# Layer 0's front in another order: twelve convolution taps and the norms' sums of squares on TensorE, other blocks' norms later

## The chip, the cores and the metric

The kernel runs on one core of a Trainium2 chip. The time of a run is the device time of one execution in microseconds (us). Engines are named as in the profile: PE is TensorE's matmuls, PEld its weight loads, DVE is VectorE, ACT is ScalarE, POOL is GpSimd, SP the queue that issues the DMAs.

## What is computed

Two layers of a streaming encoder, on 1024 prompt frames and 8 x 16 sample frames of 1024 channels:

```
h = rms_norm(x, g1)                          # x * rsqrt(mean(x*x) + eps) * g
q, k, v, a, b = split(h @ w_in)
u = a * sigmoid(b)
A = sliding_window_attention(rope(norm(q)), rope(norm(k)), v, sinks)
C = silu(layer_norm(causal_depthwise_conv31(u) + conv_b))
x = x + concat(A * beta_a, C * beta_c) @ w_out
h = rms_norm(x, g2)
x = x + square(relu(h @ w_up)) @ w_down
```

The depthwise convolution has 31 taps and 512 channels: each output column is the sum of 31 shifted columns of `u`, each times one weight per channel, plus a bias. Everything is float32.

## The kernel before

Channels lie on the 128 partitions and frames along the free axis. The 1152 frames are three blocks (`b` = 0, 1, 2) of 384; the last holds the sample frames. A product of the projections is made of three matmuls per 128 rows (`gemm`, L213 to L215): weights and activations are each split into a rounded float32r part and a rest, and hi x hi, hi x lo and lo x hi are summed. A unit is one 128-column piece of a projection, 24 such matmuls; its weights come in two half units (`half_unit`), each a DMA into one of four `raw` tiles, a cast on ScalarE (L205) and a subtraction on GpSimd (L206), here called a split, into one of six `w` tiles.

A layer's front does, for each block: `rmsnorm`; `glu` (8 units for a and b, then `u` on GpSimd); `make_qkv` (6 units); the attention in chunks of 64 queries (scores L525, softmax on VectorE and ScalarE, transposes L550, values L560); the convolution (`conv`); `out` (8 units of the output projection `w_out`, and the second norm); then the feed-forward network. Attention and convolution are generators that stand in lanes beside the projections; after every unit `tick` advances them by the rates in `ATT` and `CONV`, and a list scheduler then sets each engine's order. Every engine works off its queue in order.

The convolution runs on VectorE alone. For each of 4 channel tiles a PSUM tile `c` takes 31 taps, one instruction each (L345 for the first, with the bias, then L347), and ScalarE copies it back over `u` (L350). `conv_tail` makes the layer norm of it, with one fp32 matmul for the mean (L651) and three for the variance.

`rmsnorm` squares pairs of 128-channel rows on ScalarE (L260) into tiles `f`, of which there are two, adds them on VectorE (three of L264, then L265), and sums over the partitions with three matmuls by a column of ones (L241). `rsqrt` makes the inverse root of 128 x 3 numbers on GpSimd: a power (L231) and four small steps (L232 to L235). Three transposes spread it over the partitions (L247), and VectorE and ScalarE write the normalised block in two parts (L275, L276, L277).

In layer 0 the order is: load blocks 0 and 1, norms of both; `glu` of block 0 (its convolution starts beside it); norm of block 2; `make_qkv` of 0 and 1; attention of 0 to its end, then of 1 beside what follows; `glu` of 1 and 2; `out` of 0 with its second norm; feed-forward of block 0 in the background; `make_qkv` of 2; and on. It is in `run`:

Of the kernel before, what the change touches and what calls it, by code (L numbers as in the profile page):

```python
# [37 lines left out]
CONV = ((6, 5, 3), (3.5, 3.5, 3.5))  # L38
TAIL = (3, 2)
ATT = ((0.5, 0.3, 0.3), (0.3, 0.35, 0.25))  # L40
# [21 lines left out]
class Kernel:  # L62
# [160 lines left out]
    def rsqrt(self, v, shape, scale=1.0):  # L223
# [8 lines left out]
        nc.gpsimd.tensor_tensor(out=t, in0=y, in1=v, op=ALU.mult)  # L232
        nc.gpsimd.tensor_tensor(out=t, in0=t, in1=y, op=ALU.mult)
        nc.gpsimd.tensor_scalar(out=t, in0=t, scalar1=-0.5 * scale, scalar2=1.5 * scale, op0=ALU.mult, op1=ALU.add)
        nc.gpsimd.tensor_tensor(out=r, in0=t, in1=y, op=ALU.mult)  # L235
# [14 lines left out]
    def rmsnorm(self, x, l, gcol):  # L250
        for h in self.rmsnorm_steps(x, l, gcol):
            pass
        return h

    def rmsnorm_steps(self, x, l, gcol):
# [9 lines left out]
        nc.vector.tensor_tensor(out=acc[:, 0], in0=acc[:, 0], in1=acc[:, 1], op=ALU.add)  # L265
        yield
        R, spare = self.pr()
        r = self.token_rsqrt(spare[:, :NB], acc[:, 0], C_O1024)
# [57 lines left out]

    def conv(self, l, b):
# [3 lines left out]
        for ct in range(4):  # L331
# [8 lines left out]
            for k in range(CW):  # L340
# [8 lines left out]
                if k == CW - 1:  # L349
                    nc.scalar.copy(u[:, :BT], acc)  # L350
# [663 lines left out]
    def run(self):  # L1014
# [10 lines left out]
        x.append(self.load_x(src[1]))  # L1025
        h1 = [self.rmsnorm(x[b], 0, G1) for b in range(2)]
        for l in range(DEPTH):
# [16 lines left out]
            def out(b):  # L1044
# [3 lines left out]
                if b < NB - 1:  # L1048
                    h[b] = self.rmsnorm(x[b], l, G2)

            with tc.tile_pool(name=f"ap{l}", bufs=1) as self.ap:
# [3 lines left out]
                if l == 0:  # L1055
                    for n in ("sk", "sv", "sc"):
                        self.after(nc.sync.dma_start(a[n + "o"], a[n + "old"]), self.mark)
                    h1.append(self.rmsnorm(self.load_x(src[2]), l, G1))
                attention(0, self.make_qkv(l, 0, h1[0]))
                if l:  # L1060
                    self.glu(l, 1, h1[1], conv)
                qf = self.make_qkv(l, 1, h1[1])
                self.finish("attention")
                attention(1, qf)
                if not l:
                    self.glu(l, 1, h1[1])
                    self.side("conv", self.conv(l, 1), conv[1])
                if l:
# [192 lines left out]
```

## Time and profile before

| | us |
|---|---|
| median of 3 runs (2408.23 to 2409.8) | 2408.95 |
| the profiled execution | 2407.56 |
| its span, first to last instruction | 2405.8 |
| TensorE busy in the span | 2319.9 (96%) |
| VectorE busy | 1658.2 (69%) |
| ScalarE busy | 1270.5 (53%) |
| GpSimd busy | 1530.3 (64%) |

Busy is the share of the span in which an engine worked on at least one instruction. The busy time of TensorE contains stretches at a lower granted clock: its clock has two levels, 1.2 and 2.4 GHz, and the profile gives the mean granted share of the higher one. In a timeline a row is an instruction or a run of like ones: start, length, engine, line, operation, output<-input, shape, count, and in brackets the idle time of the engine before it and what ended it. A plain fp32 matmul leaves two records.

### The profile page before, as it was taken

How to read it: one execution, taken by the hardware profiler on the slowest of the kernel's cores; microseconds unless marked ns; L12 is line 12 of the kernel's file. 1: busy time of each engine (PE TensorE's matmuls, PEld its weight loads, DVE VectorE, ACT ScalarE, POOL GpSimd, SP SyncE). 2: the span in 40 equal slices, each digit the busy share in tenths (PEclk: the TensorE clock that was granted, in tenths of full speed). 3: DMA queues.
4: the chain of work that ended last, by engine and by line, in shares of the span. 5: the costliest groups of instructions: out<-in, count | busy, mean ns of one | idle time of the engine just before them, and what ended most of it. 6: DMA issues, size and time to landing. Idle time of an engine off the chain costs nothing.

```text
span 2405.8 us, 38983 instructions
## 1 busy us (share of the span) xinstructions
PE 2319.9 (96%) x13822; PEld 2254.8 (94%) x13822; DVE 1658.2 (69%) x2993; ACT 1270.5 (53%) x2732; POOL 1530.3 (64%) x1375
## 2 busy tenths in 40 slices
PE   6999898999999999999999999999999999999999
PEld 6898798999998999999999999999999899999999
DVE  4999887996368777686687764599834877752222
ACT  5467555555435555554566467466443555544442
POOL 5885566566467666766865776856445666676662
PEclk9999899999999999999999999999999999999999
DMA  5422433334332222544333344334333122244442
GB/s 179 139 92 93 122 96 110 111 107 138 110 97 78 68 71 80 164 122 134 101 119 108 114 155 134 128 105 124 97 101 118 55 70 75 84 162 136 132 127 75
DMA packets 164260, 266.49 MB, mean 111 GB/s; under 512 B 24753, under 2 KB 55729, under 8 KB 164017
## 3 DMA queue, kind: packets, MB, share of 16 engines
q1 hardware_dynamic: 164064, 264.01, 35.5%
q8 instruction: 108, 1.77, 0.3%
q14 instruction: 88, 0.71, 0.1%
HBM read 250.19 MB, written 16.05 MB: 111 GB/s over the span
## 4 chain that ended last, share of the span: by engine, by line
PE 76%; DVE 16%; POOL 3%; issue 2%; DMA 2%; ACT 2%; SPq 0%; DVEq 0%; POOLq 0%; ACTq 0%
PE g L715 14%; PE g L213 13%; PE g L215 13%; PE g L214 13%; DVE c L347 5%; PE x L998 4%; PE x L918 4%; PE g L998 3%; PE g L918 2%; PE m L715 2%; PE r L715 2%; POOL w L885 1%; PE c L715 1%; DMA A<-in_w 1%; PE s L525 1%
## 5 line engine op out<-in xcount | busy, mean ns | idle before, releaser
L206 POOL TENSOR_TENSOR w<-raw,w 128x512 fp32r<-128x512 f32 x728 | 965.6, 1336 | 592.3 <-ACT w L205 572.7
L205 ACT CAST w<-raw 128x512 fp32r<-128x512 f32 x728 | 445.6, 620 | 457.6 <-PE g L715 134.6
L213 PE MATMUL g<-h,w 128*128 128x384 f32 x1696 | 576.4, 340 | 7.2 <-ACT h L276 3.8
L214 PE MATMUL g<-h,w 128*128 128x384 f32 x1696 | 573.1, 338 | 1.1 <-DVE h L277 1.1
L215 PE MATMUL g<-h,w 128*128 128x384 f32 x1696 | 573.4, 338 | 0.0
L347 DVE SCALAR_TENSOR_TENSOR c<-u,vec,c 128x384 f32<-128x384 f32 (+1 forms) x960 | 498.5, 519 | 19.0
L715 PE MATMUL g<-hid,w 128*128 128x384 f32 x2304 | 431.2, 341 | 9.3 <-DVE x L717 6.3
L715 PEld LDWEIGHTS g<-hid,w 128*128 128x128 f32 x2304 | 399.6, 189 | 17.8 <-DVE x L717 10.8
L213 PEld LDWEIGHTS g<-h,w 128*128 128x128 f32 x1696 | 320.8, 189 | 11.4 <-ACT h L276 4.6
L214 PEld LDWEIGHTS g<-h,w 128*128 128x128 f32 x1696 | 320.6, 189 | 2.8 <-DVE h L277 2.0
L215 PEld LDWEIGHTS g<-h,w 128*128 128x128 f32 x1696 | 320.4, 189 | 0.7
L699 DVE TENSOR_TENSOR hid<-t,hid 128x384 fp32r<-128x384 f32 x128 | 106.3, 831 | 197.4 <-ACT hid L698 197.2
L885 POOL TENSOR_TENSOR w<-S,w 128x512 fp32r<-128x512 f32 x96 | 138.5, 1446 | 120.0 <-ACT w L884 119.7
L717 DVE TENSOR_TENSOR x<-x,g 128x384 f32<-128x384 f32 x240 | 129.8, 549 | 77.0 <-PE g L715 76.7
L696 ACT ACTIVATE t<-g 128x384 f32<-128x384 f32 x128 | 62.9, 491 | 143.7 <-PE g L215 142.5
L998 PE MATMUL x<-F,w 128*128 128x384 f32 x624 | 119.2, 336 | 3.4 <-DVE x L1001 2.4
L885 POOL TENSOR_TENSOR w<-raw,w 128x512 fp32r<-128x512 f32 x64 | 90.6, 1416 | 41.0 <-ACT w L884 39.7
L998 PEld LDWEIGHTS x<-F,w 128*128 128x128 f32 x624 | 109.4, 188 | 4.9 <-DVE x L1001 2.5
L998 PE MATMUL g<-F,w 128*128 128x384 f32 x528 | 108.3, 340 | 4.1 <-ACT F L807 1.4
L884 ACT CAST w<-S 128x512 fp32r<-128x512 f32 x96 | 59.7, 622 | 96.1 <-DVE S L871 51.1
L998 PEld LDWEIGHTS g<-F,w 128*128 128x128 f32 x528 | 92.6, 188 | 8.4 <-ACT F L807 2.7
L885 POOL TENSOR_TENSOR w<-A,w 128x512 fp32r<-128x512 f32 x64 | 87.0, 1364 | 18.6 <-ACT w L884 18.4
(227 smaller groups left out, 4016.8 us busy)
## 6 DMA issues: line engine op xcount, KB each, us to landing
raw<-in_w SPq DMA_DIRECT2D x792, 256.0 KB, 2.7
A<-in_w SPq DMA_DIRECT2D x64, 256.0 KB, 2.8
x<-in_x SPq DMA_DIRECT2D x24, 384.0 KB, 4.8
x<-xd SPq DMA_DIRECT2D x12, 384.0 KB, 5.2
kept<-x SPq DMA_DIRECT2D x4, 768.0 KB, 4.0
x<-kept SPq DMA_DIRECT2D x8, 384.0 KB, 4.7
xd<-x SPq DMA_DIRECT2D x4, 768.0 KB, 3.5
out_y<-x SPq DMA_DIRECT2D x4, 768.0 KB, 4.7
```

The lines of the kernel that those rows point to most:

```text
L205: nc.scalar.copy(u[:, 0], raw)
L206: nc.gpsimd.tensor_tensor(out=u[:, 1], in0=raw, in1=u[:, 0].bitcast(F32), op=ALU.subtract)
L213: nc.tensor.matmul(ps, lhsT=u(0, k), rhs=h(0, k), start=k == 0, stop=False)
L214: nc.tensor.matmul(ps, lhsT=u(0, k), rhs=h(1, k), start=False, stop=False)
L215: self.pe = nc.tensor.matmul(ps, lhsT=u(1, k), rhs=h(0, k), start=False, stop=k == KT - 1)
L347: t = nc.vector.scalar_tensor_tensor(out=o, in0=src(k), scalar=w, in1=o, op0=ALU.mult, op1=ALU.add)
L699: nc.vector.tensor_tensor(out=hid[:, 1], in0=f, in1=hid[:, 0].bitcast(F32), op=ALU.subtract)
L715: self.pe = nc.tensor.matmul(ps, lhsT=u(p), rhs=hid[:, q], start=i == 0, stop=i == n - 1)
L717: nc.vector.tensor_tensor(out=x[:, m], in0=x[:, m], in1=ps, op=ALU.add)
L885: nc.gpsimd.tensor_tensor(out=u[:, 1], in0=f[n], in1=u[:, 0].bitcast(F32), op=ALU.subtract)
L918: nc.tensor.matmul(ps, lhsT=u[:, p, k], rhs=H[h](q, k), start=start and k == 0 and i == 0, stop=k == 3 and i == 2, skip_group_check=True)
L998: nc.tensor.matmul(o, lhsT=u[:, p, 2 * i + j], rhs=F(j, hn)[:, q], start=start and n == 0, stop=n == 5, skip_group_check=True)
```

## The change

The convolution of block 0 in layer 0 does its first 12 taps on TensorE, as 12 matmuls with a diagonal matrix of the tap's weights, in two groups of six; VectorE builds the diagonals from the identity (`diagonal`) and adds the other 19 taps to the same PSUM tile; the bias moves to ScalarE's copy. In five norms of layer 0 (`pe=True`) each square is summed by TensorE, 24 matmuls by the column of ones instead of VectorE's four additions and 3 matmuls. In the first norm the four small steps behind the power run on VectorE. Block 1 is loaded and normed after `glu` of block 0, block 2 after `out` of block 0; `glu` of 1 comes before `make_qkv` of 1; `out` of 0 comes before `glu` of 2; the feed-forward of block 0 starts before `glu` of 2. The rates of attention 1 rise from 0.3 to 0.4. Layer 1 keeps its order.

```diff
+TAPS = ((12, 0, 0), (0, 0, 0))
-ATT = ((0.5, 0.3, 0.3), (0.3, 0.35, 0.25))
+ATT = ((0.5, 0.4, 0.3), (0.3, 0.35, 0.25))
...
-        nc.gpsimd.tensor_tensor(out=t, in0=y, in1=v, op=ALU.mult)
...
+        eng = eng or nc.gpsimd
+        eng.tensor_tensor(out=t, in0=y, in1=v, op=ALU.mult)
...
+        if pe:
+            R, spare = self.pr()
+            nc.vector.memset(spare[:, :NB], 0.0)
         for i in range(0, KT, 2):
             sq = self.two()
             nc.scalar.activation(sq, x[:, i:i + 2], AF.Square)
-            if acc is None:
+            if pe:
+                for k in range(2):
+                    for j in range(NB):
+                        nc.tensor.matmul(spare[:, j:j + 1], lhsT=sq[:, k, j * 128:(j + 1) * 128], rhs=self.cst[:, C_O1024:C_O1024 + 1],
+                                         start=False, stop=i + k == KT - 1, skip_group_check=True)
+            elif acc is None:
...
+    def diagonal(self, l, ct, k0):
+
+        d = self.hp.tile([128, 2, BT], F32R, tag="hid", name=self.nm("dg"), bufs=4).bitcast(F32).rearrange("p a b -> p (a b)").rearrange("p (k c) -> p k c", c=128)
+        w = self.v(l, CWT + ct * CW + k0, 6)
+        self.nc.vector.tensor_tensor(out=d, in0=self.ident.unsqueeze(1).to_broadcast([128, 6, 128]), in1=w.unsqueeze(2).to_broadcast([128, 6, 128]), op=ALU.mult)
+        self.diagonals.append(d)
...
-            for k in range(CW):
+            taps = TAPS[l][b]
+            for k0 in range(0, taps, 6):
+                if ct == 0 and k0 == 0:
+                    yield
+                dg = self.diagonals.pop(0)
+                for k in range(6):
+                    self.pe = nc.tensor.matmul(acc, lhsT=dg[:, k], rhs=u[:, k0 + k:k0 + k + BT], start=k0 + k == 0, stop=k0 + k == taps - 1)
+                if 2 * ct < 4:
+                    self.diagonal(l, ct + 2, k0)
+                yield
+            for k in range(taps, CW):
...
-        x.append(self.load_x(src[1]))
-        h1 = [self.rmsnorm(x[b], 0, G1) for b in range(2)]
+        self.diagonals = []
+        h1 = [self.rmsnorm(x[0], 0, G1, True, nc.vector)]
+        for ct in range(2):
+            for k0 in range(0, TAPS[0][0], 6):
+                self.diagonal(0, ct, k0)
...
                 if l == 0:
+                    h1.append(self.rmsnorm(self.load_x(src[1]), l, G1, True))
+                    attention(0, self.make_qkv(l, 0, h1[0]))
+                    self.glu(l, 1, h1[1])
+                    self.side("conv", self.conv(l, 1), conv[1])
                     for n in ("sk", "sv", "sc"):
                         self.after(nc.sync.dma_start(a[n + "o"], a[n + "old"]), self.mark)
...
+                    qf = self.make_qkv(l, 1, h1[1])
+                    self.finish("attention")
+                    attention(1, qf)
+                    out(0)
+                    h1.append(self.rmsnorm(self.load_x(src[2]), l, G1, True))
+                    self.back, self.mix = self.feed_forward(l, range(alone), [blk(0)]), mix[1]
+                    self.glu(l, 2, h1[2])
```

Three places show how the engines' queues change. The first is GpSimd's queue at the start, before (L231 to L235 are the first norm's power and its four steps on tiles `s`, L206 the weights' splits):

```order
L231 TENSOR_TENSOR s_120<-s_118,half 128x3
L206 TENSOR_TENSOR w_216<-raw_215,w_216 128x512
L232 TENSOR_TENSOR s_121<-s_120,s_118 128x3
L206 TENSOR_TENSOR w_221<-raw_220,w_221 128x512
L206 TENSOR_TENSOR w_250<-raw_249,w_250 128x512
L233 TENSOR_TENSOR s_121<-s_121,s_120 128x3
L206 TENSOR_TENSOR w_255<-raw_254,w_255 128x512
L206 TENSOR_TENSOR w_305<-raw_304,w_305 128x512
L234 TENSOR_SCALAR s_121<-s_121 128x3
L206 TENSOR_TENSOR w_310<-raw_309,w_310 128x512
L235 TENSOR_TENSOR s_122<-s_121,s_120 128x3
```

And with the change (the split is L207 there, the power L232):

```order
L207 TENSOR_TENSOR w_186<-raw_185,w_186 128x512
L207 TENSOR_TENSOR w_191<-raw_190,w_191 128x512
L207 TENSOR_TENSOR w_220<-raw_219,w_220 128x512
L207 TENSOR_TENSOR w_225<-raw_224,w_225 128x512
L207 TENSOR_TENSOR w_288<-raw_287,w_288 128x512
L207 TENSOR_TENSOR w_293<-raw_292,w_293 128x512
L232 TENSOR_TENSOR s_133<-s_131,half 128x3
```

The power has moved behind the first six splits, and the four steps have left this queue.

The second place is TensorE's queue where the output projection of block 0 begins (it multiplies `ao`, the attention's output; `p` and `pt` are an attention chunk's probabilities before and after the transpose, `s` the scores), with the change:

```order
L585 MATMUL m_1946<-cst,p_1918 128x128
L585 MATMUL m_1946<-cst,p_1919 128x128
L595 MATMUL m_1946<-pt_1939,v_981 128x256 x6
L595 MATMUL m_1946<-pt_1947,v_981 128x256 x3
L560 MATMUL s_2441<-k_888,q_1645 128x64 x6
L560 MATMUL s_2441<-k_1983,q_1645 128x128 x6
L214 MATMUL g_2167<-ao_1068,w_2169 128x384
L214 MATMUL g_2210<-ao_1068,w_2212 128x384
```

Before, the same projection began right behind a unit of block 2's `glu` (`h_607`) and one chunk's transposes:

```order
L214 MATMUL g_2674<-h_608,w_2715 128x384
L215 MATMUL g_2674<-h_607,w_2715 128x384
L550 MATMUL m_2026<-cst,p_2006 128x128
L550 MATMUL m_2026<-cst,p_2007 128x128
L213 MATMUL g_2769<-ao_1034,w_2771 128x384
L213 MATMUL g_2870<-ao_1034,w_2872 128x384
```

The last chunks of the first attention now stand between the last unit of block 1 and the projection that needs them, with no unit among them.

The third place is TensorE's queue after that projection, up to the next unit. Before, one norm (its sums L241, its broadcast L247) and parts of two chunks stand there, with the keys' sums (L374) of block 2's first unit; then come the feed-forward's first unit (`h_3248`) and block 2's next (`h_607`):

```order
L374 MATMUL g_3274<-cst,t_3309 128x2 x3
L241 MATMUL r_3231<-cst,f_3219 128x1 x3
L560 MATMUL m_2648<-pt_2641,v_1369 128x256 x6
L560 MATMUL m_2648<-pt_2649,v_1451 128x256 x3
L550 MATMUL m_2838<-cst,p_2818 128x128
L550 MATMUL m_2838<-cst,p_2819 128x128
L247 MATMUL r_3231<-cst,s_3239 128x128 x3
L213 MATMUL g_3331<-h_3248,w_3333 128x384
L213 MATMUL g_3377<-h_607,w_3379 128x384
```

With the change, this is the end of a piece of 41 rows without a unit, with two norms' sums (L270) and broadcasts (L249) and most of four chunks:

```order
L270 MATMUL r_2777<-cst,f_2803 128x1 x6
L595 MATMUL m_3015<-pt_3008,v_1994 128x256 x6
L595 MATMUL m_3015<-pt_3016,v_2075 128x256 x3
L249 MATMUL r_2777<-cst,s_2815 128x128 x3
L585 MATMUL m_3203<-cst,p_3183 128x128
L585 MATMUL m_3203<-cst,p_3184 128x128
L214 MATMUL g_2849<-h_2824,w_2852 128x384
L214 MATMUL g_2850<-h_2824,w_2886 128x384
L214 MATMUL g_2933<-h_2750,w_2935 128x384
```

The first unit behind it is block 2's (`h_2824`, from the second of the two norms); the feed-forward's (`h_2750`, from the first) stands behind it.

## Rows read from the trace of the kernel before

**Rows 1.** The page, busy time, share of the span, instructions.

```profile
PE 2319.9 (96%) x13822; PEld 2254.8 (94%) x13822; DVE 1658.2 (69%) x2993; ACT 1270.5 (53%) x2732; POOL 1530.3 (64%) x1375
```

**Rows 2.** Busy time by stretches: PE, PEld, DVE, ACT, POOL; granted clock, DMA share, GB/s.

```profile
0.00:25.00 25.00, 2.37 (x10) 1.88 (x10) 5.75 (x10) 9.19 (x12) 11.18 (x19) 1.00 0.68 240
25.00:190.00 165.00, 158.72 (x1021) 151.06 (x1021) 146.12 (x264) 95.30 (x219) 131.21 (x133) 0.97 0.37 119
190.00:310.00 120.00, 105.03 (x636) 97.90 (x636) 108.62 (x203) 74.45 (x184) 57.16 (x61) 0.91 0.35 102
310.00:400.00 90.00, 83.15 (x521) 77.81 (x520) 66.15 (x125) 43.66 (x84) 68.54 (x80) 0.98 0.37 115
400.00:550.00 150.00, 145.68 (x887) 140.48 (x886) 142.52 (x324) 92.11 (x257) 85.23 (x82) 0.99 0.36 109
550.00:2405.80 1855.80, 1824.96 (x10755) 1785.67 (x10754) 1189.08 (x2072) 955.75 (x1979) 1177.02 (x1001) 1.00 0.35 109
```

**Rows 3.** Timeline of the start: start us, length us, engine, line, operation.

```profile
11.30 1.44 PE L241 MATMUL r<-cst,f 128*128 128x1 f32 x6 [11.30 <-DVE f L265]
...
13.10 0.86 POOL L231 TENSOR_TENSOR s<-s,half 128x3 f32<-128x3 f32 x1 [10.23 <-DMA raw<-in_w]
13.93 1.26 POOL L206 TENSOR_TENSOR w<-raw,w 128x512 fp32r<-128x512 f32 x1
...
21.74 0.19 POOL L235 TENSOR_TENSOR s<-s,s 128x3 f32<-128x3 f32 x1
...
22.93 2.19 DVE L275 SCALAR_TENSOR_TENSOR f<-x,vec,r 128x384 f32<-128x384 f32 x4 [9.98 <-PE r L247]
...
24.98 1.33 PE L213 MATMUL g<-h,w 128*128 128x384 f32 x3 [2.09 <-ACT h L276]
```

**Rows 4.** Busy time, clock, DMA share and GB/s while the first loads run.

```profile
2.00:14.00 12.00, 1.44 (x6) 1.36 (x6) 3.68 (x6) 4.29 (x6) 1.77 (x4) 1.00 0.97 364
```

**Rows 5.** TensorE's timeline at a plain fp32 matmul among projections.

```profile
214.09 0.81 PE L651 MATMUL r<-f,cst 128*128 128x384 f32 x2
214.44 0.63 PE L215 MATMUL g<-h,w 128*128 128x384 f32 x1
214.91 0.33 PE L213 MATMUL g<-h,w 128*128 128x384 f32 x1
```

**Rows 6.** TensorE's timeline at a norm's three sums among projections.

```profile
41.32 0.72 PE L241 MATMUL r<-cst,f 128*128 128x1 f32 x6
41.90 0.42 PE L214 MATMUL g<-h,w 128*128 128x384 f32 x1
```

**Rows 7.** VectorE from 25 to 420 us, groups: count | busy us, mean ns | idle before.

```profile
L347 DVE SCALAR_TENSOR_TENSOR c<-u,vec,c 128x384 f32<-128x384 f32 x240 | 148.4, 618 | 4.3
L277 DVE TENSOR_TENSOR h<-f,h 128x768 fp32r<-128x768 f32 x16 | 17.7, 1114 | 0.1
L275 DVE SCALAR_TENSOR_TENSOR f<-x,vec,r 128x384 f32<-128x384 f32 x29 | 16.2, 609 | 9.0 <-PE r L247 8.9
...
L264 DVE TENSOR_TENSOR f<-f,f 128x768 f32<-128x768 f32 x10 | 11.7, 1168 | 3.6 <-ACT f L260 3.6
...
L265 DVE TENSOR_TENSOR f<-f 128x384 f32<-128x384 f32 x3 | 4.1, 1375 | 0.0
```

**Rows 8.** TensorE's timeline in block 0's output projection.

```profile
241.92 1.33 PE L213 MATMUL g<-co,w 128*128 128x384 f32 x3 [5.05 <-ACT co L640]
```

**Rows 9.** TensorE's timeline after that projection, at block 0's second norm.

```profile
290.31 0.38 PE L550 MATMUL m<-cst,p 128*128 128x128 f32 x2
...
293.25 1.33 PE L560 MATMUL m<-pt,v 128*128 128x256 f32 x9 [0.23 <-DVE pt L552]
295.10 0.80 PE L550 MATMUL m<-cst,p 128*128 128x128 f32 x4 [0.52 <-DVE og L564]
298.09 0.90 PE L247 MATMUL r<-cst,s 128*128 128x128 f32 x3 [2.19 <-POOL s L235]
...
301.08 1.01 PE L213 MATMUL g<-h,w 128*128 128x384 f32 x2 [1.67 <-ACT h L276]
```

More of the change, by code (lines that the diff above doesn't have):

```diff
@@ L264, in rmsnorm_steps @@
                 nc.vector.tensor_tensor(out=acc, in0=acc, in1=sq, op=ALU.add)
-        nc.vector.tensor_tensor(out=acc[:, 0], in0=acc[:, 0], in1=acc[:, 1], op=ALU.add)
+        if not pe:
+            nc.vector.tensor_tensor(out=acc[:, 0], in0=acc[:, 0], in1=acc[:, 1], op=ALU.add)
         yield
-        R, spare = self.pr()
-        r = self.token_rsqrt(spare[:, :NB], acc[:, 0], C_O1024)
+        if pe:
+            r = self.rsqrt(self.plus_eps(spare[:, :NB], [NB]), [NB], eng=eng)
+        else:
+            R, spare = self.pr()
+            r = self.token_rsqrt(spare[:, :NB], acc[:, 0], C_O1024)
         yield
@@ L349, in conv @@
                 if k == CW - 1:
-                    nc.scalar.copy(u[:, :BT], acc)
+                    if taps:
+                        nc.scalar.activation(u[:, :BT], acc, AF.Identity, bias=self.v(l, CB + ct))
+                    else:
+                        nc.scalar.copy(u[:, :BT], acc)
                 yield
@@ L1048, in out @@
                 if b < NB - 1:
-                    h[b] = self.rmsnorm(x[b], l, G2)
+                    h[b] = self.rmsnorm(x[b], l, G2, not l)
             with tc.tile_pool(name=f"ap{l}", bufs=1) as self.ap:
@@ L1055, in run @@
                 if l == 0:
+                    h1.append(self.rmsnorm(self.load_x(src[1]), l, G1, True))
+                    attention(0, self.make_qkv(l, 0, h1[0]))
+                    self.glu(l, 1, h1[1])
+                    self.side("conv", self.conv(l, 1), conv[1])
                     for n in ("sk", "sv", "sc"):
                         self.after(nc.sync.dma_start(a[n + "o"], a[n + "old"]), self.mark)
-                    h1.append(self.rmsnorm(self.load_x(src[2]), l, G1))
-                attention(0, self.make_qkv(l, 0, h1[0]))
-                if l:
-                    self.glu(l, 1, h1[1], conv)
[L1062 to L1068, printed above, removed]
+                    qf = self.make_qkv(l, 1, h1[1])
[5 more added lines that the diff above has]
+                    self.glu(l, 2, h1[2])
+                else:
+                    attention(0, self.make_qkv(l, 0, h1[0]))
+                    self.glu(l, 1, h1[1], conv)
+                    qf = self.make_qkv(l, 1, h1[1])
+                    self.finish("attention")
+                    attention(1, qf)
                     out(0)
@@ L1072, in run @@
                     self.glu(l, 2, h1[2])
-                else:
-                    self.glu(l, 2, h1[2])
-                    out(0)
-                self.back, self.mix = self.feed_forward(l, range(alone), [blk(0)]), mix[1]
+                    self.back, self.mix = self.feed_forward(l, range(alone), [blk(0)]), mix[1]
+                if l == 0:
+                    self.finish("attention")
                 qf = self.make_qkv(l, 2, h1[2])
```

14 lines of the change are left out of this document (7 added, 7 removed).

## The prediction

> **What bounds the kernel now.** I read the page first: TensorE is busy 96% of the span, the next engine 69% [rows 1]. Then the table by stretches [rows 2], which shows where the missing time lies. Before 25 us TensorE does nearly nothing. From 550 us on it is busy 1825 of 1856 us at a granted clock of 1.00, one matmul every 0.17 us (1855.8 over 10755): whatever is late at 550 us is late at the end, one for one. Between 25 and 550 us, the part that the change rewrites, it is idle 6.3 + 15.0 + 6.9 + 4.3 = 32.4 us, and the granted clock falls short by 0.03 x 165 + 0.09 x 120 + 0.02 x 90 + 0.01 x 150 = 19.1 us. So some 51.5 us are all that any reordering of this part can give back. In the same stretches VectorE is full: 146.1 + 108.6 of the 285 us from 25 to 310, 89%. That is what the change relieves, and it does so by giving TensorE more work.
>
> **The change, part by part.**
>
> *The start.* Before, the four small steps after the power (`L232` to `L235`) stand on GpSimd between weight splits of 1.26 us each, so that 8.6 us pass from the power at 13.10 to the last step at 21.74, and the first product of the norm on VectorE starts at 22.93 [rows 3]. The change moves these four to VectorE, each some 0.2 us, but the power itself now stands behind six splits. The splits wait for weights, and the DMA engines are full until the weights come: 0.97 of 16 engines from 2 to 14 us [rows 4]. Without the second block's 1.57 MB at 364 GB/s ahead of them the weights come 4.3 us earlier; the fifth and sixth still wait for a raw buffer. I put the sixth split's end at 16, the power's at 17, four steps and the broadcast at 18.9: **-4 us**. The squares' sums run on TensorE, idle then; at the half clock a record takes 0.24 us (1.44 us for six [rows 3]), so 48 of them take 11.5 us from the arrival of the constants at some 7.5 us, and the gain would be 0.5; with sums and weights both early it is 6.
>
> *Taps on TensorE.* 4 channel tiles x 12 = 48 matmuls of 128x384 in plain fp32. The nearest row has just this form, the mean of the convolution's tail: two records, and from its start to the projection after the next 0.82 us, of which the projection between takes its usual 0.17: 0.65 us [rows 5]. 48 x 0.65 = **+31 us**, in the stretch where TensorE has projections to do; nothing covers it. The upper bound has half of them behind waits, at 1.2 GHz, where each takes twice: 24 x 0.65 + 24 x 1.3 = 47 us. Nothing in the rows makes one cheaper.
>
> *Sums on TensorE.* 24 matmuls instead of 3 in each of five norms. Six records took 0.58 us at full clock, 0.10 each [rows 6]; half of the 0.24 at half clock is 0.12. I take 0.11: 48 records are 5.3 us against 0.6, 4.7 more. The first norm's lie in the idle start, two lie in the stretch after the first output projection (below), and two cost in full: **+9.4 us** (8 to 10).
>
> *VectorE's relief.* 48 taps x 0.618, and for each norm 3 x 1.168 + 1.375 = 4.9 us [rows 7]; eight diagonals of 128x768 come back at about 1.1 each (by the sum of two 768 wide tensors in the same rows; 0.9 to 1.2), four of them in the empty start. From 25 to 310 us that is 30 + 15 - 4 = 40 us less of 255: VectorE falls from 89% to about 75%. This is worth nothing by itself, only as TensorE's waits on VectorE grow shorter.
>
> *The order.* The first output projection now comes after four groups of projections, not five: block 2's (8 units, 24 matmuls each) follows it. Two places of TensorE's queue change.
> (a) Ahead of the output projection nothing but attention is left. Before, it began between projections and then waited 5.05 us for the convolution's output, and its next three products took 1.33 us, at half clock [rows 8]. That wait goes: the tail now ends well ahead. In its place stand the last two chunks of the first attention. A chunk's end, from its last transposes to the next one's first, took 4.8 us when TensorE had little else (290.31 to 295.10 [rows 9]); two such ends and their first transposes take about 12 us, of which some 7 are matmuls that have to be done anyway: **+5 us** (3 to 10).
> (b) After it, two norms follow each other and TensorE's first product is block 2's, which needs the second. Before, one norm stood there and 10.8 us passed from the last product of the projection before to the next (290.31 to 301.08), 7.8 of it up to the broadcast at 298.09 [rows 9]. Now: 7.8 to the first broadcast; then the products of the first norm, 8 x 0.609 + 4 x 1.114 = 9.3 us of VectorE [rows 7], hold the two tiles that the second norm's squares need; then again 7.8 and 3.0: 28 us. Against 10.8 that is 17 more. Three chunks' attention products run in it, which before lay among projections: 1.33 us for the product with the values and 0.8 for four transposes [rows 9], about 6 us in all. The two norms' sums are inside it too: **+11 us** (5 to 17).
>
> *What comes back.* Of the 51.5 us I leave 2 for the cold start of the first products (1.33 us for three, from 24.98 [rows 3]) and 8 for that norm's stall, which (b) counts. 41 remain: waits on VectorE or on the convolution's tail [rows 8], and the half clock behind them. With a quarter of VectorE free instead of a tenth, I let three quarters go: **-30 us** (20 to 45).
>
> *Against the skill.* Busy time of matmuls, by which I counted the slack, shows TensorE 32.4 us idle from 25 to 550 us, the weight loads' column (PEld) 165 - 151.1 + 120 - 97.9 + 90 - 77.8 + 150 - 140.5 = 57.7 [rows 2]. The Trainium skill ("Perfetto Trace Analysis", Identifying the Most-Contended Engine) says that matmul busy time is a bad measure and that the weight loads' share is a good one. By it there would be 25 us more to give back, and at the same share the sum would be 15 us lower. The trace speaks for most of the smaller figure: after 550 us, where TensorE is full, PEld too is idle 3.8% of the time, which is 20 us in 525.
>
> **Sum.** -4 + 31 + 9.4 + 5 + 11 - 30 = +22.4. The profiled execution took 2407.56 us (span 2405.8), so it comes to 2430; the median of the three runs is 1.4 higher, 2408.95, which gives **2431 us**. Adding the terms' bounds in quadrature (3 at the start, 6 for taps, 12 for what comes back, 6 and 3 for the two stretches) gives some 15 either way for this case alone, 2417 to 2446.
>
> **Rivals.** About 0.2%, 4.8 us, is what a measurement of this kernel can tell from no change.
> - *VectorE was the true limit (faster).* It is 89 to 95% busy in the stretches from 25 to 310 us and from 400 to 550 us, and a tap ahead in its queue holds up the softmax behind it. If all of TensorE's slack but the cold start returned (49 us) and the two new stretches cost no more than the old ones: -4 + 31 + 9.4 - 49 = -12.6, 2396 us. It decides only if over 36 us come back beside free stretches; TensorE would then be full from 21 us on, which it is in no stretch before 400 us [rows 2]. Against it speaks the queue order: both new stretches are chains through VectorE, ScalarE and GpSimd. 0.10.
> - *The sides cancel.* 45 us come back, (a) costs 3, (b) 5: +0.4, 2409 us. 0.10.
> - *More slack than TensorE's row shows* (the weight loads' measure above): 15 us lower, 2416 us. 0.05.
> - *The new order waits more than I count.* The chains of (a) and (b) reach their upper bounds, 10 and 17, and only 20 come back: -4 + 31 + 9.4 + 10 + 17 - 20 = +43, 2452 us. 0.05.
> - That the change doesn't do what it says is excluded: the queues hold 48 taps and 153 - 48 = 105 more sums.
>
> **How the numbers follow.** My forecast has 0.70. Faster by over 0.2% is the first rival, 0.10; within 0.2% the second, 0.10; the forecast, the third and the fourth are slower, 0.80. The range leaves out the first rival and the outer part of the last, 2408 to 2450.
>
> **What would show it.** In the profile after: the first projection at about 21 us; 96 records of the taps at 0.32 us from one to the next in full streams; TensorE's busy sum about 45 to 50 us higher; VectorE's about 45 lower; a stretch of some 28 us after the output projection of block 0 without a projection; the wait on the convolution's output there gone. The stretch from 400 us on should only be shifted. I am wrong if TensorE's idle and cold time up to 550 us falls under 20 us, or if the taps run in fewer than 0.65 us each.

## The result, and the profile after

The changed kernel takes **2452.8 us** (median of 4 runs, 2448.28 to 2455.11), the kernel before 2409.19 in the same comparison: a ratio of **1.0176, 95% interval 1.0164 to 1.0188**, 43.6 us slower. Forecast was 2431 with a range of 2408 to 2450. The direction was right, and the size was half of what came. The profiled execution has a span of 2451.6 us.

The page's busy line of the changed kernel answers to [rows 1]:

```profile
PE 2390.3 (97%) x14128; PEld 2316.6 (94%) x14128; DVE 1610.7 (66%) x2942; ACT 1273.5 (52%) x2732; POOL 1525.8 (62%) x1371
```

TensorE is busy 70 us more (forecast 45 to 50), VectorE 47.5 us less (forecast 45). The same stretches as in [rows 2], with the same columns:

```profile
0.00:25.00 25.00, 12.55 (x55) 11.86 (x56) 9.96 (x17) 9.72 (x13) 12.50 (x16) 1.00 0.67 226
25.00:190.00 165.00, 165.00 (x959) 147.65 (x959) 105.73 (x193) 78.43 (x182) 99.80 (x102) 0.99 0.29 98
190.00:310.00 120.00, 106.35 (x645) 98.63 (x643) 85.92 (x182) 71.07 (x179) 52.62 (x55) 0.74 0.26 86
310.00:400.00 90.00, 88.28 (x518) 87.37 (x517) 63.10 (x96) 45.66 (x86) 57.78 (x58) 0.99 0.38 114
400.00:550.00 150.00, 148.80 (x934) 140.68 (x932) 100.39 (x235) 79.07 (x181) 97.60 (x106) 0.98 0.34 111
550.00:2451.60 1901.60, 1869.35 (x11027) 1830.39 (x11026) 1245.60 (x2222) 989.55 (x2096) 1205.53 (x1034) 1.00 0.33 109
```

Up to 190 us TensorE is full, as it was in no such stretch before, and VectorE is far from it (64%). Counted as the prediction counted it, the slack from 25 to 550 us is 16.6 us of idle time and 0.01 x 165 + 0.26 x 120 + 0.01 x 90 + 0.02 x 150 = 36.8 us that the clock falls short, 53 us together, against 51.5 before (32.4 idle, 19.1 of clock). In sum no slack has gone. It was spread before, and now most of it lies between 190 and 310 us, where the granted clock is 0.74.

Two pieces of TensorE's queue without a unit are there. The first is (a), ahead of block 0's output projection. TensorE's timeline:

```profile
207.74 0.34 PE L216 MATMUL g<-h,w 128*128 128x384 f32 x1
...
212.69 1.01 PE L585 MATMUL m<-cst,p 128*128 128x128 f32 x4
218.56 0.69 PE L585 MATMUL m<-cst,p 128*128 128x128 f32 x2 [4.86 <-DVE pt L587]
...
220.74 2.29 PE L595 MATMUL m<-pt,v 128*128 128x256 f32 x9
...
228.95 2.29 PE L595 MATMUL m<-pt,v 128*128 128x256 f32 x9 [1.25 <-DVE pt L587]
...
234.20 1.01 PE L214 MATMUL g<-ao,w 128*128 128x384 f32 x2
```

It lasts 26.3 us (forecast 12). The second is (b), between that projection and block 2's first unit, 42.1 us (forecast 28):

```profile
271.31 0.34 PE L216 MATMUL g<-co,w 128*128 128x384 f32 x1
...
272.43 2.34 PE L270 MATMUL r<-cst,f 128*128 128x1 f32 x18
...
287.76 0.90 PE L249 MATMUL r<-cst,s 128*128 128x128 f32 x3
...
291.38 2.29 PE L595 MATMUL m<-pt,v 128*128 128x256 f32 x9 [2.30 <-DVE pt L587]
...
297.43 5.28 PE L270 MATMUL r<-cst,f 128*128 128x1 f32 x24 [0.30 <-ACT f L266]
...
303.04 5.12 PE L270 MATMUL r<-cst,f 128*128 128x1 f32 x24
...
310.57 0.90 PE L249 MATMUL r<-cst,s 128*128 128x128 f32 x3 [0.29 <-POOL s L237]
...
313.57 0.79 PE L214 MATMUL g<-h,w 128*128 128x384 f32 x3 [1.42 <-ACT h L291]
```

The two norms follow each other as forecast: the second broadcast (L249) comes 22.8 us after the first. The table by stretches for just these two shows what they cost:

```profile
208.00:234.20 26.20, 17.26 (x123) 14.37 (x122) 19.86 (x47) 12.58 (x35) 17.82 (x23) 0.59 0.14 48
271.50:313.50 42.00, 36.79 (x196) 33.84 (x195) 22.93 (x58) 27.30 (x73) 5.49 (x13) 0.55 0.21 69
```

The second looks 88% busy, but at a granted clock of 0.55, that is almost all of it at 1.2 GHz. Idle time plus (1 - clock) x busy is 16.0 us in (a) and 21.8 in (b).

The start, on the engines of the first norm, answers to [rows 3]:

```profile
8.08 10.37 PE L270 MATMUL r<-cst,f 128*128 128x1 f32 x48 [8.08 <-DMA cst<-in_cst]
...
18.96 0.85 POOL L232 TENSOR_TENSOR s<-s,half 128x3 f32<-128x3 f32 x1
...
20.45 0.16 DVE L237 TENSOR_TENSOR s<-s,s 128x3 f32<-128x3 f32 x1
...
23.72 0.69 PE L214 MATMUL g<-h,w 128*128 128x384 f32 x1 [2.16 <-ACT h L291]
```

The sums wait for the constants and then take 0.22 us a record, to 18.45. That is the pace that the same records have from 297.43 us on, where the granted clock is 0.50. The table's clock of 1.00 up to 25 us does not fit this pace, here and in [rows 2]; the times follow the pace. The first product comes at 23.7, 1.3 us earlier than before.

### The profile page after: what moved, and what is told of

Read it like the earlier page. It is cut to its first block, busy times and chain, and to the rows that moved or that the text cites. A ratio compares the mean times of both kernels' runs of the same rounds, so it can differ in the third digit from the quotient of the medians.

```text
span 2451.6 us, 39551 instructions
## 1 busy us (share of the span) xinstructions
PE 2390.3 (97%) x14128; PEld 2316.6 (94%) x14128; DVE 1610.7 (66%) x2942; ACT 1273.5 (52%) x2732; POOL 1525.8 (62%) x1371
## 4 chain that ended last, share of the span: by engine, by line
PE 78%; DVE 9%; POOL 2%; issue 1%; DMA 1%; ACT 1%; DVEq 0%; SPq 0%; POOLq 0%; ACTq 0%
PE g L750 14%; PE g L214 13%; PE g L216 13%; PE g L215 13%; PE x L1033 5%; PE x L953 4%; PE g L1033 3%; PE g L953 2%; PE m L750 2%; PE r L750 2%; DVE c L379 2%; PE c L750 1%; PE s L560 1%; POOL w L920 1%; PE m L595 1%
## 5 line engine op out<-in xcount | busy, mean ns | idle before, releaser
L207 POOL TENSOR_TENSOR w<-raw,w 128x512 fp32r<-128x512 f32 x728 | 961.8, 1331 | 617.3 <-ACT w L206 597.8
L206 ACT CAST w<-raw 128x512 fp32r<-128x512 f32 x728 | 445.7, 620 | 482.1 <-PE g L750 129.1
L379 DVE SCALAR_TENSOR_TENSOR c<-u,vec,c 128x384 f32<-128x384 f32 (+2 forms) x916 | 471.0, 514 | 35.8 <-PE c L368 16.9
L920 POOL TENSOR_TENSOR w<-A,w 128x512 fp32r<-128x512 f32 x64 | 86.8, 1360 | 17.8 <-ACT w L919 17.6
```

The costliest lines, as they stand in the source:

```text
L206: nc.scalar.copy(u[:, 0], raw)
L207: nc.gpsimd.tensor_tensor(out=u[:, 1], in0=raw, in1=u[:, 0].bitcast(F32), op=ALU.subtract)
L379: t = nc.vector.scalar_tensor_tensor(out=o, in0=src(k), scalar=w, in1=o, op0=ALU.mult, op1=ALU.add)
L920: nc.gpsimd.tensor_tensor(out=u[:, 1], in0=f[n], in1=u[:, 0].bitcast(F32), op=ALU.subtract)
```

## The experiments

Eighteen kernels ran. Times are medians. Each has its ratio to the kernel before, run beside it on the same chip, and differences between runs are differences of these ratios, times 2409. An interval is about 0.1 to 0.2% wide on either side, so a difference is good to some 5 us. "Loss" is, for one profile, TensorE's idle time plus (1 - granted clock) x busy, added over 46 windows of 15 us from 30 to 720 us: 48.9 us before, 50.6 after.

### The order and the work apart

**The order alone.**

```diff
-TAPS = ((12, 0, 0), (0, 0, 0))
+TAPS = ((0, 0, 0), (0, 0, 0))
-h1 = [self.rmsnorm(x[0], 0, G1, True, nc.vector)]
+h1 = [self.rmsnorm(x[0], 0, G1)]
```

and likewise without `True` (or `not l`) in the other norms.

> The changed order without its work: no taps and no sums on TensorE, the first norm's steps on GpSimd. Theory 'order' (most of the 44 us are the two stretches of TensorE's queue without projections, the last chunks of the first attention and then two norms in a row; taps and sums are nearly paid back by shorter waits on VectorE): the stretches stand here too, so 2430 to 2450 us. Theory 'work' (the 50 us of added matmuls are the cost, and the new order costs nothing): 2400 to 2413 us.

It took 2422.55 us, ratio 1.0064 (1.0047 to 1.0081): +15 us, between the two theories. Stretch (a) is 51.8 us here, with the convolution's tail and a fourth chunk in it, (b) is 34.2, and the loss 66.7. The raised rate of attention 1 counts as part of the order here; it was not run alone.

**The work in the old order**: `run` as before, but for

```diff
-        h1 = [self.rmsnorm(x[b], 0, G1) for b in range(2)]
+        self.diagonals = []
+        h1 = [self.rmsnorm(x[b], 0, G1, True, (nc.vector, None)[b]) for b in range(2)]
+        for ct in range(2):
+            for k0 in range(0, TAPS[0][0], 6):
+                self.diagonal(0, ct, k0)
```

and `True` or `not l` in the other norms.

> The work of the change in the order of before: 12 taps and the squares' sums on TensorE, the first norm's four steps on VectorE, rates and order as before. Theory 'order': taps 31 and sums outside waits some 10 to 15 us, against some 30 us of waits and half clock that come back and 1 to 3 at the start: 2405 to 2425 us. Theory 'work': 2440 to 2455 us.

It took 2456.16 us, 1.0191 (1.0176 to 1.0206): +46 us. The theory of the order, as I had stated it, falls: without the new order the work costs as much as the whole change. But the loss is 51.9, so this order too kept its slack.

**The change without taps.**

```diff
-TAPS = ((12, 0, 0), (0, 0, 0))
+TAPS = ((0, 0, 0), (0, 0, 0))
```

> The changed kernel with all 31 taps on VectorE again. Theory 'order': TensorE loses 31 us of work and VectorE, ahead of the same two stretches, gets 30 us more to do, so the waits that the taps had removed are back: 2440 to 2460 us, no gain. Theory 'work': 31 us less, 2415 to 2425 us.

It took 2436.43 us, 1.0115 (1.01 to 1.013). The taps cost the change 15 us, half of what their records take. Step by step, the order costs 15.4 us, the sums and the first norm 12.3 and the taps 14.7; that these make the 42.4 us of the ratio is so by construction, and another sequence of steps prices them otherwise (below).

**Without the sums in stretch (b)**, and in block 1's second norm.

```diff
-                    h[b] = self.rmsnorm(x[b], l, G2, not l)
+                    h[b] = self.rmsnorm(x[b], l, G2)
...
-                    h1.append(self.rmsnorm(self.load_x(src[2]), l, G1, True))
+                    h1.append(self.rmsnorm(self.load_x(src[2]), l, G1))
```

> The changed kernel with the sums of the two norms that follow block 0's output projection back on VectorE; the first two norms keep theirs on TensorE. If the 48 matmuls of these sums, at half clock some 0.22 us each, are what made that stretch 42 us long instead of 28: some 10 us less, 2440 to 2445 us, and the stretch about 32 us. If the chain of squares, tiles and broadcasts sets its length whoever adds: 2449 to 2457 us, and the stretch 38 to 46 us.

It took 2446.49 us, 1.0156 (1.0141 to 1.0172), 5 us less than the change, which is just what a difference is good for, and (b) is 35.3 us. So 7 of the 14 us by which (b) outlasted the forecast are the sums themselves, at half clock inside the chain.

### What the relief of VectorE is worth

**Taps alone in the old order.** The diff is that of the work in the old order, without `True` in the norms and without `nc.vector`.

> The kernel before with the 12 taps on TensorE and nothing else: order, rates, norms and sums as before. If the relief of VectorE pays half of the taps back wherever they stand: 2420 to 2428 us. If it pays nothing in this order (the taps' 31 us stay): 2436 to 2444 us. What is missing to the 2456 us of the run with the sums too is the price of the sums.

It took 2441.44 us, 1.0125 (1.0104 to 1.0146): +30 us, the taps' full price. No relief shows, but TensorE's queue has a new piece without a unit, of which the next run tells. In this sequence the steps are 30.1 us for the taps, 15.9 for sums and first norm (to the work in the old order) and -3.6 for the order.

**Taps on no engine, old order.**

```diff
-            for k in range(CW):
+            first = 12 * (l == 0 and b == 0)
+            for k in range(first, CW):
...
-                    if k == 0:
+                    if k == first:
```

> The kernel before with the first 12 taps of block 0's convolution in layer 0 left out altogether, on no engine (the bias stays). VectorE is relieved of 30 us and TensorE gets nothing for it. If TensorE's waits in the front are waits on a full VectorE, 15 to 30 us come back: 2379 to 2394 us. If they are chains that a free VectorE does not shorten: 2399 to 2411 us.

It took 2420.21 us, 1.0032 (1.0021 to 1.0043): less work, and 8 us **slower**. TensorE's timeline has a new piece of 30 us:

```profile
142.96 0.51 PE L561 MATMUL m<-pt,v 128*128 128x256 f32 x3
...
145.46 0.91 PE L652 MATMUL r<-f,cst 128*128 128x384 f32 x2
...
152.96 1.44 PE L241 MATMUL r<-cst,f 128*128 128x1 f32 x6 [0.68 <-DVE f L659]
...
156.69 0.90 PE L247 MATMUL r<-cst,s 128*128 128x128 f32 x3 [0.76 <-POOL s L235]
159.43 1.55 PE L383 MATMUL r<-cst,s 128*64 128x128 f32 x12 [1.84 <-DVE u L663]
...
168.63 1.44 PE L438 MATMUL g<-cst,t 128*64 128x2 f32 x12 [1.66 <-ACT t L434]
...
173.13 0.69 PE L213 MATMUL g<-h,w 128*128 128x384 f32 x1 [0.61 <-DVE s L439]
```

The convolution ends 12 taps earlier, so its tail (L652, L241, L247) now falls between the first two units of block 1's `glu`, with attention chunks beside it. The keys' broadcast (L383) writes the same tile `r`, of which there is one, and comes after the tail; the queries' sums (L438) and the next unit come after that. The runs with taps in the old order have the same piece, 35 and 32 us long.

**Taps on no engine, new order**: the same two lines in the changed kernel, with `TAPS` zero.

> The changed kernel with the same 12 taps left out altogether, the rest of the change in place. Against the 2436 us with all 31 taps on VectorE, the relief alone, and against the 2453 us of the change, the taps' matmuls alone. If the matmuls cost what the records say, 31 us: 2419 to 2424 us, so that the relief in the new order is worth some 15. If the relief is worth nothing here either: 2432 to 2438 us, and the matmuls cost only 16.

It took 2437.35 us, 1.0104 (1.0084 to 1.0123), as long as with all 31 taps on VectorE (1.0115), within what a difference is good for. By the ratios the relief alone returns 3 of 30 us. By the two profiles it returns 7.6 us up to the last twelve products `g<-hid` ahead of 760 us (they start at 741.87 instead of 749.43), of which 1.6 are left at the end of the span; where the rest goes was not traced. By the ratios the matmuls cost 17 us of their 31.

**The tail moved, taps left out**, in the old order.

```diff
-CONV = ((6, 5, 3), (3.5, 3.5, 3.5))
+CONV = ((3.7, 5, 3), (3.5, 3.5, 3.5))
```

> The kernel before with the 12 taps left out, as in the run that took 7 us more than before, and the rate of block 0's convolution lowered from 6 to 3.7 steps a unit, so that its 76 steps last as many units as the 124 did. In that run the convolution's tail stood between two units of block 1's glu, in a piece of 30 us without a unit; in this queue that piece is gone. If the tail's place swallowed the relief: 20 to 30 us come back, 2383 to 2400 us. If VectorE's relief is worth nothing wherever the tail stands: 2406 to 2418 us.

It took 2414.5 us, 1.0011 (1.0 to 1.0022). The piece of 30 us is gone and 5 us came back, but the kernel is still no faster than before, with 30 us of VectorE's work gone. The second expectation holds: the relief is worth nothing. The loss is 54.7. TensorE's waits from 25 to 550 us agree: those that an instruction of VectorE ended add up to 17.4 of 34.2 us before, and to 25.3 of 35.7 us here. So before the change half of the waits ended with another engine, and those on VectorE did not shrink with its work. The longest ones before (us in total, times, longest):

```profile
PE g L213 <- ACT co L640: 6.9, 2, 5.1
PE m L550 <- DVE pt L552: 4.5, 3, 2.8
PE g L213 <- ACT h L276: 3.8, 2, 2.1
```

And in this run:

```profile
PE g L213 <- DVE s L439: 5.9, 2, 3.1
PE g L716 <- DVE x L718: 3.6, 3, 2.0
PE g L213 <- ACT h L276: 3.6, 2, 2.1
```

**All the work in the old order, tail moved.**

```diff
-CONV = ((6, 5, 3), (3.5, 3.5, 3.5))
+CONV = ((4.0, 5, 3), (3.5, 3.5, 3.5))
```

> All the work of the change in the order of before, which took 2456 us, with the rate of block 0's convolution lowered from 6 to 4 steps a unit, so that its tail stands behind block 1's glu; the piece of TensorE's queue of 32 us with tail and chunks and no unit is gone. If the tail's place swallowed the relief: 2425 to 2440 us. If the work is the whole cost: 2448 to 2460 us.

It took 2442.62 us, 1.0129 (1.0114 to 1.0143): 15 us less than with the piece of 32 us, just above the first forecast. The loss is 29.4 us, 19.5 less than before the change, the lowest of all.

**The same without the taps' matmuls**: `TAPS` zero, the 12 taps on no engine as above, rate 3.7.

> The work of the change in the order of before with the convolution's rate at 3.7, but the 12 taps left out altogether instead of standing on TensorE: sums on TensorE and the first norm's steps on VectorE stay. Against the 2443 us of the run with taps and sums at a rate of 4, the difference is what the taps' matmuls cost where no stretch without units lies beside them. If they cost their 31 us in full: 2410 to 2414 us. If half of them fill waits that are there anyway: 2422 to 2430 us. Against the 2414 us of the run without taps and sums, the difference is the price of the sums: 10 to 19 us by their records in the second case, nothing in the first.

It took 2424.01 us, 1.0064 (1.005 to 1.0078), loss 48.4. So the taps' matmuls cost 16 us and bring the loss down by 19: about half of them run in time that TensorE loses anyway. They fill waits, while the relief, which both runs have, did not shorten them. Sums and first norm cost 13 us here (1.0064 against 1.0011).

### The two stretches

**Block 2's norm early.**

```diff
+                    h1.append(self.rmsnorm(self.load_x(src[2]), l, G1, True))
                     qf = self.make_qkv(l, 1, h1[1])
                     self.finish("attention")
                     attention(1, qf)
                     out(0)
-                    h1.append(self.rmsnorm(self.load_x(src[2]), l, G1, True))
```

> The changed kernel with block 2's load and norm moved ahead of the second block's keys and queries, so that one norm, not two, follows block 0's output projection, and block 2's units are ready there. If the two stretches of TensorE's queue without units are the loss, the second shrinks from 42 us to 10 to 15: 2430 to 2438 us. If the attention's chains only stand uncovered in another place: 2447 to 2456 us.

It took 2435.8 us, 1.0107 (1.0093 to 1.012), 17 us less than the change. Stretch (b) breaks into two of 4.8 and 4.4 us, (a) is 21.5. As expected.

**And `glu` of block 2 ahead of the output projection.**

```diff
                     attention(1, qf)
+                    self.glu(l, 2, h1[2])
                     out(0)
                     self.back, self.mix = self.feed_forward(l, range(alone), [blk(0)]), mix[1]
-                    self.glu(l, 2, h1[2])
```

> The changed kernel with block 2's norm early and its eight units ahead of block 0's output projection, where they stood before; taps, sums and the rest as changed. If the two stretches without units are the loss, both go: 2415 to 2428 us. If some 50 us of the front are lost in every order, by attention chunks that follow one another with nothing beside them: 2445 to 2458 us.

It took 2440.45 us, 1.0124 (1.011 to 1.0139). No stretch over 12 us is left and the loss is 35.4, but the kernel is no faster than the last. With (b) gone, or both stretches, taps and sums cost 26 to 31 us over the kernel before (these two runs and the one with all the work and the tail moved).

**The first attention faster.**

```diff
-ATT = ((0.5, 0.4, 0.3), (0.3, 0.35, 0.25))
+ATT = ((0.7, 0.4, 0.3), (0.3, 0.35, 0.25))
```

> The changed kernel with the rate of the first attention raised from 0.5 to 0.7 chunks a unit, so that its chunks stand beside more of block 1's units and fewer are left for the stretch ahead of the output projection. If those left-over chunks are the loss there (26 us, 16 of them lost): 2438 to 2446 us. If not, or if the list scheduler puts them at the same place: 2449 to 2457 us.

It took 2453.63 us, 1.0182 (1.0169 to 1.0195): nothing. Stretch (a) is 26.8 us. The rate is not what leaves the chunks there.

### The first norm

**The first norm alone**, in the old order, its sums on TensorE and its steps on VectorE.

```diff
-        h1 = [self.rmsnorm(x[b], 0, G1) for b in range(2)]
+        h1 = [self.rmsnorm(x[b], 0, G1, not b, (nc.vector, None)[b]) for b in range(2)]
```

> The kernel before with the first norm alone changed: its squares summed on TensorE, the four steps behind its power on VectorE; the second block is loaded as before, all later norms and the taps as before. By the first product of the changed kernel, 1.3 us earlier than before with the second block's load later too: 2405 to 2409 us. If the sums' half clock and the constants eat it up: 2409 to 2412 us.

It took 2405.94 us, 0.9971 (0.9958 to 0.9984), 7 us faster, though its first product came at 26.95, 2 us *later* than before. Its loss from 30 to 705 us is 7 us smaller; by which step, this run does not settle.

**The four steps alone**, with the sums left on VectorE:

```diff
-        return self.rsqrt(self.plus_eps(ps, [NB]), [NB])
+        return self.rsqrt(self.plus_eps(ps, [NB]), [NB], eng=eng)
```

with `eng=nc.vector` handed down from the call of the first norm only.

> The kernel before with one edit: in the first norm the four small steps behind the power run on VectorE; its sums stay on VectorE, everything else as before. The power stands ahead of the splits here, as before. If the first product waits for these steps alone: power's end at 14.0 us, four steps of 0.2, broadcast at 15.5, first product at some 18.5 instead of 25.0: 2401 to 2404 us. If the weights' first splits hold it: first product at 20 to 22, 2404 to 2407 us. If the gain at the start is lost again behind it: 2407 to 2411 us.

It took **2399.18 us, 0.9952 (0.994 to 0.9965)**, 11.5 us faster than before, with a few lines of the change. By its median it is the fastest kernel of this study; the last two below lie within 3 us of it. The first product came at 22.3, not 18.5. The timeline of GpSimd and VectorE shows why:

```profile
13.50 0.86 POOL L232 TENSOR_TENSOR s<-s,half 128x3 f32<-128x3 f32 x1 [10.63 <-DVE s L221]
14.33 4.92 POOL L207 TENSOR_TENSOR w<-raw,w 128x512 fp32r<-128x512 f32 x4
14.40 1.22 DVE L234 TENSOR_TENSOR s<-s,s 128x3 f32<-128x3 f32 x1 [1.05 <-POOL s L232]
15.65 1.19 DVE L235 TENSOR_TENSOR s<-s,s 128x3 f32<-128x3 f32 x1
16.87 1.19 DVE L236 TENSOR_SCALAR s<-s 128x3 f32<-128x3 f32 x1
18.10 1.18 DVE L237 TENSOR_TENSOR s<-s,s 128x3 f32<-128x3 f32 x1
```

Each small step ends within 0.1 us of the end of one of GpSimd's four splits (4.92 us for four, 1.23 each), and takes 1.2 us where it took 0.16 in the changed kernel, in which the splits were over by then.

**The splits held behind the steps.** On top of the last kernel, the first eight splits depend on the last step (`self.first`, `self.held = 8`), so that the first in GpSimd's queue waits for it.

```diff
-        nc.gpsimd.tensor_tensor(out=u[:, 1], in0=raw, in1=u[:, 0].bitcast(F32), op=ALU.subtract)
+        i = nc.gpsimd.tensor_tensor(out=u[:, 1], in0=raw, in1=u[:, 0].bitcast(F32), op=ALU.subtract)
+        if self.held:
+            self.held -= 1
+            self.tc.add_manual_dep(i.ins, self.first.ins.name, mybir.DependencyInfo(mybir.DependencyClass.Sync, mybir.DependencyReason.DATA), reason="held")
```

> The kernel before with the first norm's four steps on VectorE, and GpSimd's first splits held behind the last of them. In the run without the hold the steps took 1.2 us each while GpSimd split weights, against 0.16 in the change, where it did not. If the split beside them is the cause: steps of 0.16 to 0.2, first product at 18 to 19 us instead of 22.3, and 3 to 4 us less than that run's 2399: 2394 to 2397 us. If it is not, or if the later splits then hold the products: 2398 to 2403 us.

It took 2409.28 us, 0.9991 (0.9982 to 0.9999). The cause is shown by the rows, the gain is not there:

```profile
13.06 0.86 POOL L235 TENSOR_TENSOR s<-s,half 128x3 f32<-128x3 f32 x1 [10.19 <-DVE s L224]
13.95 0.16 DVE L237 TENSOR_TENSOR s<-s,s 128x3 f32<-128x3 f32 x1 [1.04 <-POOL s L235]
...
14.54 0.16 DVE L240 TENSOR_TENSOR s<-s,s 128x3 f32<-128x3 f32 x1
...
17.76 1.01 PE L217 MATMUL g<-h,w 128*128 128x384 f32 x2 [2.10 <-ACT h L294]
```

The steps take 0.16 us and the first product comes at 17.8, 7.2 us earlier than before. By 102 us it is lost: TensorE waits 4.3 us for a tile `r` behind block 2's norm, in a piece of 12.8 us without a unit (7.5 before).

**That norm moved behind block 0's keys and queries**, with and without the hold.

```diff
-                    h1.append(self.rmsnorm(self.load_x(src[2]), l, G1))
                 attention(0, self.make_qkv(l, 0, h1[0]))
+                if not l:
+                    h1.append(self.rmsnorm(self.load_x(src[2]), l, G1))
```

> The kernel before with the first norm's steps on VectorE, the splits held behind them, and block 2's load and norm moved behind block 0's keys and queries. Without that move the first product came at 17.8 us and the gain was lost: TensorE waited 4.3 us for a keys' broadcast that stood behind that norm's products on VectorE, in a stretch of 12.8 us without a unit. If that norm is what ate the gain: 2396 to 2402 us. If the loss moves on: 2405 to 2411 us.

It took 2400.47 us, 0.9964 (0.9951 to 0.9978). The 7 us of the start are there again: with the hold, the norm was what ate the gain.

> The same move of block 2's norm without the hold, on the run with the four steps on VectorE alone, which took 2399 us. If the norm costs TensorE a wait there too: 2393 to 2397 us. If not: 2397 to 2403 us.

It took 2400.97 us, 0.9966 (0.9953 to 0.9978): without the hold the move brings nothing (+3 us, within what a difference is good for).

### The runs side by side

Times over the kernel before come from the ratios; (a) and (b) are lengths without a unit ahead of block 0's output projection and behind it. The last two columns split the loss.

| run | over before, us | (a), us | (b), us | loss, us | in (a), (b) | elsewhere |
|---|---|---|---|---|---|---|
| the kernel before | 0 | none | 10.8 | 48.9 | 6.8 | 42.1 |
| the change | +42 | 26.3 | 42.1 | 50.6 | 16.0, 21.8 | 12.8 |
| its order alone | +15 | 51.8 | 34.2 | 66.7 | 35.1, 22.2 | 9.4 |
| order and sums, no taps on TensorE | +28 | 47.8 | 37.7 | 68.7 | 30.1, 19.0 | 19.6 |
| the same, taps on no engine | +25 | 41.5 | 40.9 | 60.0 | 25.8, 19.2 | 15.0 |
| block 2's norm early | +26 | 21.5 | 4.8, 4.4 | 39.1 | 13.6, 2.7 | 22.8 |

The order alone, in which VectorE has all its old work, takes the loss elsewhere from 42.1 to 9.4 us and puts 57 us into the two stretches. It moves the waits; it does not remove them. Its rows of (a) and (b) in the table by stretches:

```profile
159.70:211.40 51.70, 30.19 (x176) 24.22 (x174) 45.18 (x93) 29.05 (x77) 22.27 (x30) 0.55 0.13 46
251.20:285.40 34.20, 20.02 (x112) 16.26 (x111) 27.32 (x64) 26.29 (x73) 5.62 (x13) 0.60 0.24 85
```

With the taps on TensorE, (a) is 15 to 25 us shorter and loses 10 to 19 us less, and that is where their price comes half back. The place of the convolution's tail does not explain it: its mean stands at 164 us in the change and at 119 us with the taps on no engine, far ahead of (a) in both, and (a) is 26 us in the one and 41.5 in the other. What the rows show is that the last unit ahead of (a) ends at 208 us with the taps and at 160 to 175 without, and that (a) then holds three chunks' products with the values instead of four. So more of the chunks ran beside units; no run takes this apart further. Between the fourth and the fifth row the relief alone lowers the loss by 9 us and the time by 3.

## Why the prediction was wrong

It named the right direction and the right places, and missed 20 us of 42. The runs for the order alone, then with the sums, then with the taps give a measure for each step in that sequence.

- **Taps, +31: right as work.** 24 records lie between 42.55 and 49.99 us in TensorE's timeline, 7.44 us, so 29.8 us for four channel tiles. That is 0.62 us a tap, just under the 0.65 below which the prediction called itself wrong. The rows:

```profile
42.55 7.91 PE L368 MATMUL c<-u,dg 128*128 128x384 f32 x24
49.99 0.63 PE L216 MATMUL g<-h,w 128*128 128x384 f32 x1
```

- **What comes back, -30: the step that failed.** The prediction read VectorE as full (89%) and TensorE's lost time as waits on it, and let three quarters go by VectorE's relief, as a gain apart from the order. Leaving the taps out altogether, on any engine, returned next to nothing in three runs (+8, +3 and -3 us), and TensorE's waits on VectorE were 17.4 us before and 25.3 without the taps. As a number the 30 us came out, by luck: outside (a) and (b) the change loses 12.8 us, 29 less than before. But the order alone, without any relief, loses 9.4 there. The new order empties the old waits into (a) and (b), so their going is no gain to set against them: in all 50.6 us are lost, against 48.9 before. What does come back with the taps in place, some 12 to 15 us of their 30, comes because their matmuls run in time that TensorE loses anyway. Taps and return together were forecast at +1; the change without taps shows +15.
- **(a) +5 and (b) +11: too low, (a) above all.** In the change the two lose 16.0 and 21.8 us, where the prediction left 5, and 11 on top of the 8 of the old stall. That the order alone costs +15 against these 16 is luck: it loses 57 us there and 33 less elsewhere. The prediction priced (a) by two chunk ends of 4.8 us, where three chunks' products with the values stand, without the wait of 4.86 for the transposed probabilities and with the chunks partly at full clock. It priced (b) by [rows 9], where 3 fp32 sums stood, not 24.
- **Sums, +9.4 for two norms and nothing for two: too low.** With the start they were +5.4; the runs show 12 and 13 us. The sums inside (b) are not hidden there: without them (b) is 7 us shorter and the kernel some 5 us faster. Some 11 us in (a), 3 in (b) and 7 here come to about the 20 us that were missed, as far as losses of one profile can be added to differences of ratios.
- **The start, -4: -1.3.** The bounds held it, -0.5 to -6. The sums ran from 8.08 to 18.45 at 0.22 us a record, as the lower bound had it.
- **The whole.** With as much time lost as before, the change costs what it adds: 29.8 us of taps and, at 0.10 us a record [rows 6], some 17 us for 84 more sums behind the start, 47 us by this estimate; the profile's span is 45.8 us longer.
- **The rivals.** The one with 0.05, "the new order waits more than I count", gave 2452 and is nearest in time, though its account (all of (a) and (b) at their bounds, 20 us back) has the right sign and not the right parts. The sum of "the sides cancel" is -0.6, not +0.4; nothing hangs on it. VectorE as the true limit is refuted by the runs without taps. More slack, by the weight loads' row, would have made the change 15 us cheaper than forecast, and it came out dearer. The Trainium skill ("Perfetto Trace Analysis", Identifying the Most-Contended Engine) takes the weight loads' share, not matmul busy time, for a measure of TensorE's headroom; as a measure of what this edit could win, the runs do not bear it out.

**What stays open.** Why a piece of TensorE's queue without units forms in one order and not in another is the list scheduler's choice. That tile `r` holds the units is read from the queue and the rows of one run; giving it a second buffer was not tried. And of the 11.5 us that the four steps alone win, the earlier first product is 2.7 and a smaller loss from 30 to 705 us another 5; at which waits, was not traced. (To 720 us that loss is only 3 smaller: a wait of TensorE for weights that ends at 723.1 us before ends at 713.2 in the faster kernel, inside the last window.)

## What to carry to other kernels

A busy engine beside an idle one does not show that the idle one waits for it: leave the suspected work out for one run before moving it to the engine that bounds the kernel. A new order can empty waits in one place into another, so add up what is lost over the whole part before counting the waits that go as a gain. In a kernel with a fixed order per engine, ending one chain earlier can put its tail in a worse place, so look in the bounding engine's queue for pieces without its main work, and price them at the clock that such pieces get. Take a change of several parts apart as well: here a few lines of it were worth 11 us by themselves, inside a change that cost 44.

## What the runs showed of the hardware

GpSimd held VectorE up on tiny operations: a 128x3 step on VectorE took 1.18 to 1.22 us beside GpSimd's 128x512 subtractions and 0.16 us without them, and ended with them. The Trainium skill ("SBUF — State Buffer", SBUF: two separate sides) says that GpSimd and VectorE, the latter for operations with two inputs in SBUF or in a two-port mode, share a pair of ports that one instruction holds to its end, while the other blocks. The trace agrees, down to the step's length, 1.2 us being one split.

A stretch in which TensorE's row is 88% busy, 36.79 of 42.0 us, had a granted clock of 0.55. The records there are the narrow sums and the chunk's products, which at 1.2 GHz take 0.22 us a record and 2.3 us for nine. So the busy share alone did not tell what this stretch cost.
